# Transpositions of the heads: full-array sets at five places, or pairs on two row halves in one run

## The chip, the cores and the metric

One core of one Trainium2 chip runs the whole program. The metric is device time in microseconds, the median over the runs of one kernel; lower is better.

## The reference, cut to what matters

One decoder layer over 512 tokens with a model width of 2048: a branch of windowed attention beside a branch of gated DeltaNet, merged by gates. The change lies in the DeltaNet branch, which has 16 key heads and 32 value heads of 128 channels:

```python
d_qkv = causal_conv_silu(d_qkv, conv_w)
dq, dk, dv = jnp.split(d_qkv, [DN_KEY, 2 * DN_KEY], axis=-1)
...
dq = jnp.repeat(l2_norm(dq.reshape(B, T, DN_K_HEADS, DN_HEAD_K)), rep, axis=2)
dv = dv.reshape(B, T, DN_V_HEADS, DN_HEAD_V)
...
o = gated_delta_rule(dq, dk, dv, g, beta)
o = rms_norm(o, dn_norm_w) * jax.nn.silu(dz.reshape(B, T, DN_V_HEADS, DN_HEAD_V).astype(f32))
y_b = o.reshape(B, T, DN_VAL).astype(x.dtype) @ w_o_dn
```

`gated_delta_rule` works in chunks of 64 tokens: it inverts a triangular matrix per chunk and head and scans the chunks with a 128x128 state. Everything is float32.

## The kernel before, in words

**The stream.** The projections are computed channel by token: `channel_tile` makes one 128x512 tile of the output as 16 steps of three products each (`mm3`, lines 273 to 275: high part by high, high by low, low by high, 48 products of 128x512). Every second step calls `pump`, which advances all work that runs beside the stream; a tile so has 8 pumps, and 6 products lie between two pumps. The weights arrive by DMA as 1 MB tiles `raw` and are split in halves into a high part `whi` (cast, ScalarE, line 61) and a low part `wlo` (subtraction, VectorE, line 62); three halves are held, and a half lasts 24 products.

**The heads.** `delta_heads` goes through 16 groups, each of one key head with its two value heads. A group has five tiles of the stream: query, two values, two gates z. What follows on a tile is a Python generator (`queries`, `values`, `zgate`, and `scan` behind `queries`) that issues instructions and gives a number of pumps to wait with `yield`. [...]

**What is transposed.** The convolution leaves the query `yq` and the values `yv` as channels by tokens. `transpose4` (line 320) turns a 128x512 tile with four TensorE transpositions of 128x128: the data is the loaded operand, the identity `ident` the moving one. The query is transposed (`ptq`) only for the sum of its squares, ScalarE's `sumsq` (`junk`, line 793). The values (`ptv`) are scaled by `knorm` on ScalarE (line 927) into `vt`, four instructions for each value head. The scan's result `osb` (tokens by channels, two heads) is transposed back (`pto`) and multiplied by the gates `zh` on VectorE (line 1082), then stored to `o_d`. That makes five sets of four per group: one query, two values, two outputs.

**The block products.** `pu` holds products of 64x64 blocks that complete the inverse for a pair of chunks of 64 (lines 987, 988, 882). They run on four 64x64 tiles of the array at once: a matrix of float32 is two instructions, so a group has 32 of them. `block_copy` moves half of the result to `Y` for the next group.

**The scan.** For each of four pieces of 128 tokens: `pp` (state by key), `r`, `pv` (line 1026), its copy `vn` on ScalarE (line 1028), `vs` on VectorE (line 1033), then the products into `pod` (lines 1041, 1044, 1045) and from it the new state `S`, the copy `osb` and its squares.

**PSUM.** Each bank holds 128x512 float32. Two are for the stream, three for the pool `ptp` (transpositions, `pqk`, `pu`) and three for `psc` (the scan).

Of the kernel before, what the change touches and what calls it, by code (L numbers as in the profile page):

```python
# [7 lines left out]
F32 = mybir.dt.float32  # L8
F32R = mybir.dt.float32r
I32 = mybir.dt.int32  # L10
AF = mybir.ActivationFunctionType
ALU = mybir.AluOpType
AX = mybir.AxisListType
PSUM = bass.MemoryType.PSUM
DRAM = bass.MemoryType.DRAM

P = 128
T = 512
D = 2048
KT = D // P  # L20
NTB = T // P
EPS = 1e-6
KH = 16
VH = 32
QH = 32
HD = 64
# [19 lines left out]
class Layer:  # L46
# [653 lines left out]
    def delta_heads(self):  # L700
        tc, nc = self.tc, self.nc
        with ExitStack() as sb:
            self.ptp = sb.enter_context(tc.tile_pool(name="ptph", bufs=3, space=PSUM, reuse_waits="tile"))
            self.psc = sb.enter_context(tc.tile_pool(name="psch", bufs=3, space=PSUM, reuse_waits="tile"))
            self.gwk = sb.enter_context(tc.tile_pool(name="gwkh", bufs=1, reuse_waits="tile"))
            wk = sb.enter_context(tc.tile_pool(name="dnB", bufs=2, reuse_waits="tile"))
            self.tt = []
            for n in range(4):
                t = wk.tile([P, NTB, P], F32, tag=f"tt{n}", name=f"tt{n}", bufs=1)
                nc.gpsimd.memset(t[HD:P, :, 0:HD], 0.0)  # L710
                self.tt.append(t)
            while not self.solved:
                self.step_slow(self.solves)
            self.Y = None
            self.go(self.first_blocks(wk), 1)
            ws = sb.enter_context(tc.tile_pool(name="wsum", bufs=1, reuse_waits="tile"))
            sums = None
            for g in range(KH):
                if g == 3:
                    sums = self.paced(self.weight_sums(ws), 2.0)  # L720
                if g == 7:
                    self.drain_slow(self.solves)
                self.heads(wk, g)
            for j in range(9, 12):
                self.merge_gate("ma", j, self.ma_d)
            self.drain_live()
            self.drain_slow(sums)
# [156 lines left out]
    def block_copy(self, wk, pu):  # L884
# [2 lines left out]
        self.nc.vector.tensor_copy(out=Y[HD:P], in_=pu[1][HD:P])  # L887
        self.nc.vector.tensor_copy(out=Y[0:HD], in_=pu[0][HD:P])

    def first_blocks(self, wk):  # L890

        blk = self.block_load(wk, 0)
        yield 6
        pu = [self.ptp.tile([P, NTB, HD], F32, tag="tp", name="pu") for _ in range(2)]
        for c in range(NTB):
            self.block_product(pu, blk, c)
        self.block_copy(wk, pu)
# [9 lines left out]

    def zgate(self, wk, ps, st):
        nc = self.nc
        zh = wk.tile([P, T], F32, tag="z", name="zh", bufs=2)  # L910
        nc.scalar.activation(zh, ps, AF.Copy, scale=self.dnwh)
        th = wk.tile([P, T], F32, tag="th", name="zth")
        nc.scalar.activation(th, ps, AF.Tanh, scale=0.5)
        yield 1
        nc.vector.scalar_tensor_tensor(out=zh, in0=th, scalar=1.0, in1=zh, op0=ALU.add, op1=ALU.mult)
        st["z"].append(zh)

    def values(self, wk, g, e, ps, st):
        nc = self.nc
        y = wk.tile([P, T], F32, tag="y", name="yv", bufs=3)  # L920
        yield from self.conv(wk, ps, 32 + 2 * g + e, y)
        yield 3
        pt = self.ptp.tile([P, T], F32, tag="tp", name="ptv")
        self.transpose4(pt, lambda c: y[:, c * P : (c + 1) * P])
        vt = wk.tile([P, NTB, P], F32, tag="vt", name="vt", bufs=3)
        for c in range(NTB):
            nc.scalar.activation(vt[:, c, :], pt[:, c * P : (c + 1) * P], AF.Copy, scale=self.knorm[:, c, g : g + 1])
        st[f"v{e}"] = vt

    def queries(self, wk, g, ps, st):  # L930

        nc = self.nc
        sl = lambda c: slice(c * P, (c + 1) * P)
        q = wk.tile([P, T], F32, tag="y", name="yq", bufs=3)
        yield from self.conv(wk, ps, g, q)
        M = [self.decay_load(wk, 2 * g + e) for e in range(2)]
        kT = wk.tile([P, T], F32, tag="kT", name="kT")
        nc.sync.dma_start(out=kT, in_=self.kT_d[g])
        yield 2
        pt = self.ptp.tile([P, T], F32, tag="tp", name="ptq")  # L940
        self.transpose4(pt, lambda c: q[:, sl(c)])
        ss = self.sumsq(wk, pt)
        yield 3
        epsq = wk.tile([P, NTB], F32, tag="epsq", name="epsq")
        nc.vector.tensor_scalar(out=epsq, in0=ss, scalar1=EPS, scalar2=EPS * P, op0=ALU.add, op1=ALU.mult)
        yield 1
        for e in range(2):
            self.decay_mask(M[e])
        masks = self.last_mask
        ts1 = wk.tile([P, NTB, HD], F32, tag="ts1", name="ts1", bufs=1)  # L950
        qd, TT = [], []
        for e in range(2):
            h = 2 * g + e
            qe = wk.tile([P, NTB, P], F32, tag="qe", name="qe", bufs=2)
            nc.sync.dma_start(out=qe.rearrange("p c i -> p (c i)"), in_=self.eg_rows[h].partition_broadcast(P))
            qd.append(qe)
            b, hl = h // 16, h % 16
            t = self.tt[h % 4]
            for k2 in range(2):
                s = slice(k2 * HD, (k2 + 1) * HD)  # L960
                nc.sync.dma_start(out=t[s, :, s], in_=self.ts_d[b, k2, hl].rearrange("c j i -> j c i"))
            if e:
                nc.sync.dma_start(out=ts1[0:HD], in_=self.ts_d[b, 1, hl].rearrange("c j i -> j c i"))
            TT.append(t)
        while self.Y is None:
            yield 1
        Y = self.Y
        blk = self.block_load(wk, g + 1) if g + 1 < KH else None
        yield 3
        for e in range(2):  # L970
            self.decay_exp(M[e], 2 * g + e)
        k = wk.tile([P, NTB, P], F32, tag="k", name="k")
        nc.sync.dma_start(out=k.rearrange("p c d -> p (c d)"), in_=self.k_d[g])
        yield 1
        for e in range(2):
            qf = qd[e].rearrange("p c i -> p (c i)")
            self.behind(nc.gpsimd.tensor_tensor(out=qf, in0=qf, in1=q, op=ALU.mult), masks)  # L977
        yield 1
        pqk = self.ptp.tile([P, NTB, P], F32, tag="tp", name="pqk")
        for c in range(NTB):  # L980
            nc.tensor.matmul(pqk[:, c, :], lhsT=kT[:, sl(c)], rhs=q[:, sl(c)], start=True, stop=True)
        for e in range(2):
            nc.vector.tensor_tensor(out=M[e], in0=pqk, in1=M[e], op=ALU.mult)
        yield 4
        pu = [self.ptp.tile([P, NTB, HD], F32, tag="tp", name="pu") for _ in range(2)]
        for c in range(NTB):
            nc.tensor.matmul(pu[0][0:HD, c, :], lhsT=Y[HD:P, c, :], rhs=TT[0][HD:P, c, HD:P], start=True, stop=True)
            nc.tensor.matmul(pu[1][0:HD, c, :], lhsT=Y[0:HD, c, :], rhs=ts1[0:HD, c, :], start=True, stop=True)
            if blk:
                self.block_product(pu, blk, c)  # L990
        for e in range(2):
            nc.vector.tensor_tensor(
                out=TT[e][0:HD, :, HD:P],
                in0=pu[e][0:HD],
                in1=self.neg_beta[0:HD, :, 2 * g + e].unsqueeze(2).to_broadcast([HD, NTB, HD]),
                op=ALU.mult,
            )
        if blk:
            self.block_copy(wk, pu)
        yield 2  # L1000
        while "v1" not in st:
            yield 1
        yield 2
        yield from self.scan(wk, g, k, kT, TT, qd, M, epsq, st)

    def scan(self, wk, g, k, kT, TT, qd, M, epsq, st):
        nc = self.nc
        sl = lambda c: slice(c * P, (c + 1) * P)
        v = [st["v0"], st["v1"]]
        osb = wk.tile([P, 2, NTB, P], F32, tag="osb", name="osb", bufs=1)  # L1010
        osq = wk.tile([P, 2, NTB], F32, tag="osq", name="osq")
        S = None
        for c in range(NTB):
            if c:
                pp = self.psc.tile([P, 4, P], F32, tag="sc", name="pp")[:, 0:2, :]
                nc.tensor.matmul(pp, lhsT=kT[:, sl(c)], rhs=S, start=True, stop=True)  # L1016
                r = wk.tile([P, 2, P], F32, tag="r", name="r", bufs=1)
                for e in range(2):
                    nc.vector.scalar_tensor_tensor(
                        out=r[:, e, :], in0=pp[:, e, :], scalar=self.neg_eg[:, c, 2 * g + e : 2 * g + e + 1],  # L1020
                        in1=v[e][:, c, :], op0=ALU.mult, op1=ALU.add,
# [41 lines left out]
        z = st["z"]  # L1063
# [9 lines left out]
        for e in range(2):  # L1073
# [1 line left out]
            nc.vector.tensor_tensor(  # L1075
                out=of, in0=of, in1=ro[:, e * NTB : (e + 1) * NTB].unsqueeze(2).to_broadcast([P, NTB, P]), op=ALU.mult
            )
        yield 3
        for e in range(2):
            pt = self.ptp.tile([P, T], F32, tag="tp", name="pto")  # L1080
            self.transpose4(pt, lambda c: osb[:, e, c, :])
            nc.vector.tensor_tensor(out=z[e], in0=pt, in1=z[e], op=ALU.mult)
            yield 1
        yield 1
        for e in range(2):
# [767 lines left out]
```

## Time and profile before

| what | value |
|---|---|
| median of 3 runs | 2813.19 us (2806.18, 2813.19, 2815.07) |
| the profiled execution's own time | 2809.24 us |
| its span (first to last instruction) | 2807.4 us |
| granted TensorE clock over the span | 0.997 |
| TensorE busy | 2777.5 us |
| VectorE busy | 1951.0 us |
| ScalarE busy | 1207.4 us |
| stretch of the heads, with the tiles of the merge gate behind them | about 1018 to 2122 us |

Rows of the profile give the engine (PE TensorE products, PEld TensorE loads, DVE VectorE, ACT ScalarE, POOL GpSimd, SP the DMA queue), the line of the kernel, the operation, output<-inputs by the program's names with buffer numbers left out, the shape, and xN for a number of like instructions. In rows in order of time the first number is the start, the second how long it took, in us, and a bracket at the end gives an idle time before it with what ended it. In rows of groups the numbers behind the bar are busy us, the mean of one in ns, and behind a second bar the engine's idle time before them. For TensorE a row also has rows*columns of the array that are used. A row by stretches gives from:to, its length, then for PE, PEld, DVE, ACT and POOL the busy us and number of instructions, then the granted clock, the DMA engines' share and GB/s. A row of waits says who waited for whom, and the sum in us, the times, and the longest. Neighbouring products overlap, so what one costs in the row is told by the distance of starts.

### The profile page before, as it was taken

Reading aid. Unit: us, or ns where it says so; the run is one execution under the profiler, and the core shown is the slowest. Engines: PE = TensorE matmul, PEld = TensorE weight load, DVE = VectorE, ACT = ScalarE, POOL = GpSimd, SP = SyncE. Lnnn points to the kernel's source line nnn. Section 1 sums busy time; section 2 is a strip of 40 time slices with the busy share of each in tenths; the row PEclk is TensorE's granted clock in tenths of the full one; section 3 lists DMA queues with packets and bytes.
Section 4 is the critical chain, followed back from the end, with each engine's and each line's share of the span. In section 5 each row is a group of like instructions: output and inputs, shape, how many; then the busy total and the mean of one; then the engine's idle time right before and its main releaser. Section 6 shows DMA issues by size and latency. Waiting matters only on the chain.

```text
span 2807.4 us, 38312 instructions
## 1 busy us (share of the span) xinstructions
PE 2777.5 (99%) x14090; PEld 2271.1 (81%) x14090; DVE 1951.0 (69%) x3253; ACT 1207.4 (43%) x2508; POOL 144.3 (5%) x124
## 2 busy tenths in 40 slices
PE   8999999999999999999999999999999999999999
PEld 6788888877777778888888888888888788878887
DVE  7866976877758667678666666666657766664676
ACT  5554443244544433344534343434435454432443
POOL 0010100100100010000000000000000000000000
PEclk9999999999999999999999999999999999999999
DMA  9868763322252253367787667676657887885684
GB/s 403 350 235 252 255 237 132 111 78 98 86 165 98 91 170 119 118 210 245 248 260 251 227 234 249 222 245 221 230 184 244 305 299 248 295 274 184 243 318 165
DMA packets 228992, 603.38 MB, mean 215 GB/s; under 512 B 76706, under 2 KB 103074, under 8 KB 188482
## 3 DMA queue, kind: packets, MB, share of 16 engines
q1 hardware_dynamic: 228804, 600.93, 62.6%
q8 instruction: 111, 1.82, 0.3%
q14 instruction: 77, 0.63, 0.1%
HBM read 480.38 MB, written 118.24 MB: 213 GB/s over the span
## 4 chain that ended last, share of the span: by engine, by line
PE 89%; DMA 4%; DVE 3%; issue 1%; ACT 1%; POOL 0%; SPq 0%; DVEq 0%; POOLq 0%; ACTq 0%
PE mm L273 21%; PE mm L275 21%; PE mm L274 21%; PE m L274 5%; PE m L275 5%; PE m L273 5%; DMA E<-g_rows 1%; PE pv L1026 1%; PE pod L1045 1%; PE O L1560 1%; PE pod L1044 1%; PE pp L1016 1%; PE pod L1041 1%; DVE wlo L62 1%; DMA wa<-in_w_ada_ss 1%
## 5 line engine op out<-in xcount | busy, mean ns | idle before, releaser
L273 PE MATMUL mm<-hh,whi 128*128 128x512 f32 x2784 | 1125.7, 404 | 0.0
L275 PE MATMUL mm<-hh,wlo 128*128 128x512 f32 x2784 | 1090.1, 392 | 1.9 <-DVE wlo L62 1.9
L274 PE MATMUL mm<-hl,whi 128*128 128x512 f32 x2784 | 1087.7, 391 | 0.0
L62 DVE TENSOR_TENSOR wlo<-raw,whi 128x1024 fp32r<-128x1024 f32 x516 | 635.8, 1233 | 402.4 <-ACT whi L61 394.7
L61 ACT CAST whi<-raw 128x1024 fp32r<-128x1024 f32 x516 | 541.5, 1050 | 857.3 <-PE mm L274 613.1
L275 PEld LDWEIGHTS mm<-hh,wlo 128*128 128x128 f32 x2784 | 523.4, 188 | 116.4 <-DVE wlo L62 2.5
L273 PEld LDWEIGHTS mm<-hh,whi 128*128 128x128 f32 x2784 | 524.2, 188 | 113.8 <-issue 11.8
L274 PEld LDWEIGHTS mm<-hl,whi 128*128 128x128 f32 x2784 | 524.5, 188 | 102.2 <-issue 1.4
L1291 DVE TENSOR_TENSOR q<-q,q 128x1024 f32<-128x1024 f32 x96 | 124.6, 1298 | 0.9 <-DMA q<-in_w_out 0.9
L809 ACT ACTIVATE E<-E,neg_g 128x128 f32<-128x128 f32 x256 | 81.4, 391 | 92.7 <-POOL E L803 92.6
L847 DVE TENSOR_TENSOR A<-A,atmp 128x62 f32<-128x62 f32 (+30 forms) x124 | 107.5, 867 | 0.4
L839 DVE TENSOR_TENSOR atmp<-A 128x62 f32<-128x62 f32 (+30 forms) x124 | 106.8, 861 | 0.4
L977 POOL TENSOR_TENSOR qe<-qe,yq 128x512 f32<-128x512 f32 x32 | 52.7, 1666 | 907.2 <-DMA qe<-eg_rows 645.2
L1046 ACT COPY osb<-pod 128x256 f32<-128x256 f32 x64 | 23.8, 372 | 151.9 <-PE pod L1045 151.9
L803 POOL TENSOR_SCALAR_AFFINE_SELECT E<-E 128x512 f32<-128x512 f32 x64 | 60.0, 951 | 432.2 <-DMA E<-g_rows 367.0
L1028 ACT COPY vn<-pv 128x256 f32<-128x256 f32 x64 | 23.8, 372 | 115.5 <-PE pv L1026 115.5
L652 DVE SCALAR_TENSOR_TENSOR yv<-mm,convh,yv 128x511 f32<-128x511 f32 (+2 forms) x96 | 71.4, 743 | 1.6
L1528 ACT ACTIVATE sm<-sm,mx,rs 128x128 f32<-128x128 f32 x128 | 61.5, 482 | 3.7 <-DVE mx L1523 3.3
L1033 DVE TENSOR_SCALAR vs<-vn,kd 128x128 f32<-128x128 f32 x96 | 23.2, 283 | 53.7 <-ACT vn L1028 53.7
L472 DVE SCALAR_TENSOR_TENSOR wa<-wa,silu_cb 128x2048 f32<-128x2048 f32 x22 | 50.1, 2283 | 3.6 <-DMA wa<-in_w_ada_ss 3.6
L1056 DVE SCALAR_TENSOR_TENSOR S<-S,egl,pod 128x128 f32<-128x128 f32 x64 | 19.3, 342 | 47.9 <-ACT junk L1049 47.9
L1045 PE MATMUL pod<-vn,E 128*128 128x128 f32 x256 | 46.8, 275 | 0.0
(449 smaller groups left out, 3637.7 us busy)
## 6 DMA issues: line engine op xcount, KB each, us to landing
raw<-in_w_ch SPq DMA_DIRECT2D x158, 1024.0 KB
wa<-in_w_ada_ss SPq DMA_DIRECT2D x32, 1024.0 KB
q<-in_w_od SPq DMA_DIRECT2D x64, 512.0 KB
g_d<-q SPq DMA_DIRECT2D x64, 512.0 KB
raw<-g_d SPq DMA_DIRECT2D x32, 1024.0 KB
raw<-in_w_od SPq DMA_DIRECT2D x24, 1024.0 KB
gw<-in_w_ada_gate SPq DMA_DIRECT2D x16, 1024.0 KB
E<-g_rows SPq DMA_DIRECT2D x64, 256.0 KB
```

The lines of the kernel that those rows point to most:

```text
L61: h = self.nc.scalar.copy(out=hi, in_=src)
L62: l = self.nc.vector.tensor_tensor(out=lo, in0=src, in1=hi.bitcast(F32), op=ALU.subtract)
L273: nc.tensor.matmul(ps, lhsT=wh, rhs=xh, start=first, stop=False)
L274: nc.tensor.matmul(ps, lhsT=wh, rhs=xl, start=False, stop=False)
L275: self.last_mm = nc.tensor.matmul(ps, lhsT=wl, rhs=xh, start=False, stop=last)
L652: nc.vector.scalar_tensor_tensor(out=y[:, s:], in0=ps[:, : T - s], scalar=w[:, j : j + 1], in1=y[:, s:], op0=ALU.mult, op1=ALU.add)
L809: self.nc.scalar.activation(E[:, c, :], E[:, c, :], AF.Exp, bias=self.neg_g[:, c, h : h + 1])
L839: eng.tensor_tensor(out=t, in0=A[:, m : m + 1, m + 1 :].to_broadcast([P, m, n]), in1=A[:, :m, m : m + 1].to_broadcast([P, m, n]), op=ALU.mult,
L847: self.behind(eng.tensor_tensor(out=A[:, :m, m + 1 :], in0=A[:, :m, m + 1 :], in1=t, op=ALU.add))
L1045: nc.tensor.matmul(po[:, e, :], lhsT=M[e][:, c, :], rhs=vn[:, e, :], start=c == 0, stop=True)
L1291: self.behind(nc.vector.tensor_tensor(out=q[f], in0=q[x], in1=q[y], op=ALU.add))
L1528: nc.scalar.activation(t, t, AF.Exp, scale=r[:, h : h + 1], bias=mx[:, h : h + 1], accum_out=den[:, h : h + 1])
```

## The change

The five sets of full transpositions per group become pairs of half transpositions. `half_transposes` takes 64 rows of the data at a time: rows 0 to 63 on the upper half of the array into one PSUM bank, rows 64 to 127 on the lower half into another. Each loads 64 rows by 128 columns and moves a 64x64 identity. All of a group's sets stand in one run right behind its block products: 8 half transpositions of the query, 16 of the preceding group's outputs, 16 of the two values. Therefore:

- `values` leaves the convolved tile in `st`, and `queries` waits (in the program's order) until both value tiles and the preceding group's outputs are there.
- PSUM is shared out anew: `ptp` has two pairs of banks, `psc` two banks. `pu` and the query's halves share a pair, the outputs take both banks of `psc`.
- ScalarE reads both halves with one instruction, so their number stays: 8 scalings and 4 squares, now in one row. The product with the gates becomes four VectorE instructions of 128x256 instead of two of 128x512, and the gates get four buffers.
- The scan leaves `osb` and the gates in `outs`; the last group transposes its outputs in a run of their own.

```diff
-            self.ptp = sb.enter_context(tc.tile_pool(name="ptph", bufs=3, space=PSUM, reuse_waits="tile"))
-            self.psc = sb.enter_context(tc.tile_pool(name="psch", bufs=3, space=PSUM, reuse_waits="tile"))
+            self.ptp = sb.enter_context(tc.tile_pool(name="ptph", bufs=2, space=PSUM, reuse_waits="tile"))
+            self.psc = sb.enter_context(tc.tile_pool(name="psch", bufs=2, space=PSUM, reuse_waits="tile"))
...
+    def bank_pair(self, name):
+        return self.ptp.tile([P, 2, T], F32, tag="tp", name=name)
+
+    def half_transposes(self, dst, src, n):
+        for i in range(n):
+            for u in range(2):
+                s = slice(u * HD, (u + 1) * HD)
+                self.nc.tensor.transpose(dst(u)[:, i, :], src(i, s), self.ident[s, s])
+
+    def out_blocks(self, g):
+        osb, z = self.outs[g]
+        pt = [self.psc.tile([P, 4, P], F32, tag="sc", name="pto").rearrange("p a (b i) -> p (a b) i", i=HD) for _ in range(2)]
+        self.half_transposes(lambda u: pt[u], lambda i, s: osb[s, i // NTB, i % NTB, :], 2 * NTB)
+        return pt
+
+    def out_gates(self, g, pt):
+        osb, z = self.outs.pop(g)
+        for u in range(2):
+            for e in range(2):
+                zu = z[e].rearrange("p (c u i) -> p u c i", u=2, i=HD)[:, u]
+                self.nc.vector.tensor_tensor(out=zu, in0=pt[u][:, e * NTB : (e + 1) * NTB, :], in1=zu, op=ALU.mult)
...
-        pt = self.ptp.tile([P, T], F32, tag="tp", name="ptv")
-        self.transpose4(pt, lambda c: y[:, c * P : (c + 1) * P])
-        vt = wk.tile([P, NTB, P], F32, tag="vt", name="vt", bufs=3)
-        for c in range(NTB):
-            nc.scalar.activation(vt[:, c, :], pt[:, c * P : (c + 1) * P], AF.Copy, scale=self.knorm[:, c, g : g + 1])
-        st[f"v{e}"] = vt
+        st[f"y{e}"] = y
...
-        yield 2
-        pt = self.ptp.tile([P, T], F32, tag="tp", name="ptq")
-        self.transpose4(pt, lambda c: q[:, sl(c)])
-        ss = self.sumsq(wk, pt)
-        yield 3
...
+        while not ("y0" in st and "y1" in st and (not g or g - 1 in self.outs)):
+            yield 1
+        pair = self.bank_pair("pu")
...
+        ptq = pair[:, :, NTB * HD :].rearrange("p u (c i) -> p u c i", i=HD)
+        self.half_transposes(lambda u: ptq[:, u], lambda c, s: q[s, sl(c)], NTB)
+        pto = self.out_blocks(g - 1) if g else None
+        ptv = self.bank_pair("ptv").rearrange("p u (c i) -> p u c i", i=HD)
+        self.half_transposes(lambda u: ptv[:, u], lambda i, s: st[f"y{i // NTB}"][s, sl(i % NTB)], 2 * NTB)
...
+        if g:
+            self.out_gates(g - 1, pto)
...
-        for e in range(2):
-            pt = self.ptp.tile([P, T], F32, tag="tp", name="pto")
-            self.transpose4(pt, lambda c: osb[:, e, c, :])
-            nc.vector.tensor_tensor(out=z[e], in0=pt, in1=z[e], op=ALU.mult)
+        self.outs[g] = (osb, z)
+        if g == KH - 1:
+            yield 3
+            self.out_gates(g, self.out_blocks(g))
+        while g in self.outs:
             yield 1
```

TensorE's row of instructions in the middle of the heads, before: the second set of outputs (`pto`) with its neighbours of the stream, and further on the first value set behind the query-key products.

```order
L275 MATMUL mm<-hh,wlo 128x512
L320 MATMUL pto<-ident,osb 128x128 x4
L273 MATMUL mm<-hh,whi 128x512
L274 MATMUL mm<-hl,whi 128x512
L275 MATMUL mm<-hh,wlo 128x512
L273 MATMUL mm<-hh,whi 128x512
L274 MATMUL mm<-hl,whi 128x512
L275 MATMUL mm<-hh,wlo 128x512
L320 MATMUL pto<-ident,osb 128x128 x4
```

The same engine now, at a group's block products (the numbers behind `tt` and `ts` are buffers):

```order
L1005 MATMUL pu<-tt_9009,Y 64x64
L1006 MATMUL pu<-ts_11636,Y 64x64
L882 MATMUL pu<-ta,lab 64x64 x2
L899 MATMUL pu<-ident,yq 128x64 x8
L899 MATMUL pto<-ident,osb 128x64 x16
L899 MATMUL ptv<-ident,yv 128x64 x16
L273 MATMUL mm<-hh,whi 128x512
L274 MATMUL mm<-hl,whi 128x512
L275 MATMUL mm<-hh,wlo 128x512
```

The sets that stood each between products of the stream now follow the block products without a product of the stream between them; the query's halves are written beside `pu` and so bear its name.

ScalarE's row from the second value set to the scan's first piece, before (`zh` and `zth` belong to the gate tile, `vn`, `osb` and `junk` with `osq` to the scan):

```order
L61 CAST whi<-raw 128x1024
L927 ACTIVATE vt<-ptv,knorm 128x128 x4
L911 ACTIVATE zh<-mm,dnwh 128x512
L913 ACTIVATE zth<-mm 128x512
L1028 COPY vn<-pv 128x256
L61 CAST whi<-raw 128x1024
L1046 COPY osb<-pod 128x2x128
L1049 ACTIVATE junk,osq<-pod 128x128 x2
```

And now:

```order
L61 CAST whi<-raw 128x1024 x2
L938 ACTIVATE zh<-mm,dnwh 128x512
L940 ACTIVATE zth<-mm 128x512
L1026 ACTIVATE vt<-ptv,knorm 128x128 x8
L1035 ACTIVATE junk,ss<-pu 128x128 x4
L61 CAST whi<-raw 128x1024
L1065 COPY vn<-pv 128x256
L1083 COPY osb<-pod 128x2x128
L1086 ACTIVATE junk,osq<-pod 128x128 x2
```

Both value sets and the query's squares stand together, and the cast of a half of the weights, which stood behind the scan's first copy `vn`, stands ahead of it. VectorE's row at the same place, before:

```order
L62 TENSOR_TENSOR wlo<-raw,whi 128x1024
L915 SCALAR_TENSOR_TENSOR zh<-zth,zh 128x512
L1033 TENSOR_SCALAR vs<-vn,kd 128x128 x2
L62 TENSOR_TENSOR wlo<-raw,whi 128x1024
L1053 COPY S<-pod 128x256
```

And now (line 914 is the product of outputs and gates):

```order
L887 COPY Y<-pu 64x256
L914 TENSOR_TENSOR zh<-pto,zh 128x4x64 x4
L888 COPY Y<-pu 64x256
L942 SCALAR_TENSOR_TENSOR zh<-zth,zh 128x512
L1050 TENSOR_SCALAR epsq<-ss 128x4
L62 TENSOR_TENSOR wlo<-raw,whi 128x1024
L1070 TENSOR_SCALAR vs<-vn,kd 128x128 x2
L1090 COPY S<-pod 128x256
```

The difference of the weights (`wlo`) has moved from behind the scan's `vs` to ahead of it.

More of the change, by code (lines that the diff above doesn't have):

```diff
@@ L713, in delta_heads @@
                 self.step_slow(self.solves)
-            self.Y = None
+            self.Y, self.outs = None, {}
             self.go(self.first_blocks(wk), 1)
@@ L893, in first_blocks @@
         yield 6
-        pu = [self.ptp.tile([P, NTB, HD], F32, tag="tp", name="pu") for _ in range(2)]
+        pair = self.bank_pair("pu")
+        pu = [pair[:, u, 0 : NTB * HD].rearrange("p (c i) -> p c i", i=HD) for u in range(2)]
         for c in range(NTB):
@@ L909, in zgate @@
         nc = self.nc
-        zh = wk.tile([P, T], F32, tag="z", name="zh", bufs=2)
+        zh = wk.tile([P, T], F32, tag="z", name="zh", bufs=4)
         nc.scalar.activation(zh, ps, AF.Copy, scale=self.dnwh)
@@ L938, in queries @@
         nc.sync.dma_start(out=kT, in_=self.kT_d[g])
-        yield 2
-        pt = self.ptp.tile([P, T], F32, tag="tp", name="ptq")
-        self.transpose4(pt, lambda c: q[:, sl(c)])
-        ss = self.sumsq(wk, pt)
-        yield 3
-        epsq = wk.tile([P, NTB], F32, tag="epsq", name="epsq")
-        nc.vector.tensor_scalar(out=epsq, in0=ss, scalar1=EPS, scalar2=EPS * P, op0=ALU.add, op1=ALU.mult)
-        yield 1
+        yield 6
         for e in range(2):
@@ L978, in queries @@
         yield 1
-        pqk = self.ptp.tile([P, NTB, P], F32, tag="tp", name="pqk")
+        pqk = self.bank_pair("pqk")[:, 0].rearrange("p (c i) -> p c i", i=P)
         for c in range(NTB):
@@ L984, in queries @@
         yield 4
-        pu = [self.ptp.tile([P, NTB, HD], F32, tag="tp", name="pu") for _ in range(2)]
+        while not ("y0" in st and "y1" in st and (not g or g - 1 in self.outs)):
+            yield 1
+        pair = self.bank_pair("pu")
+        pu = [pair[:, u, 0 : NTB * HD].rearrange("p (c i) -> p c i", i=HD) for u in range(2)]
         for c in range(NTB):
@@ L997, in queries, with scan @@
             )
+        if g:
+            self.out_gates(g - 1, pto)
+        v = [wk.tile([P, NTB, P], F32, tag="vt", name="vt", bufs=3) for _ in range(2)]
+        for c in range(NTB):
+            for e in range(2):
+                nc.scalar.activation(
+                    v[e][:, c, :].rearrange("p (u i) -> p u i", u=2), ptv[:, :, e * NTB + c, :], AF.Copy,
+                    scale=self.knorm[:, c, g : g + 1],
+                )
         if blk:
             self.block_copy(wk, pu)
[L1000 to L1006, printed above, removed]
+        ss = wk.tile([P, NTB], F32, tag="ss", name="ss")
+        for c in range(NTB):
+            junk = wk.tile([P, P], F32, tag="junk", name="junk", bufs=1)
+            nc.scalar.activation(
+                junk.rearrange("p (u i) -> p u i", u=2), ptq[:, :, c, :], AF.Square, accum_out=ss[:, c : c + 1]
+            )
+        yield 3
+        yield from self.scan(wk, g, k, kT, TT, qd, M, ss, v, st)
+    def scan(self, wk, g, k, kT, TT, qd, M, ss, v, st):
         nc = self.nc
         sl = lambda c: slice(c * P, (c + 1) * P)
-        v = [st["v0"], st["v1"]]
         osb = wk.tile([P, 2, NTB, P], F32, tag="osb", name="osb", bufs=1)
@@ L1013, in scan @@
         for c in range(NTB):
+            if c == 1:
+                epsq = wk.tile([P, NTB], F32, tag="epsq", name="epsq")
+                nc.vector.tensor_scalar(out=epsq, in0=ss, scalar1=EPS, scalar2=EPS * P, op0=ALU.add, op1=ALU.mult)
             if c:
@@ L1077, in scan @@
             )
-        yield 3
-        for e in range(2):
-            pt = self.ptp.tile([P, T], F32, tag="tp", name="pto")
-            self.transpose4(pt, lambda c: osb[:, e, c, :])
-            nc.vector.tensor_tensor(out=z[e], in0=pt, in1=z[e], op=ALU.mult)
+        self.outs[g] = (osb, z)
+        if g == KH - 1:
+            yield 3
+            self.out_gates(g, self.out_blocks(g))
+        while g in self.outs:
             yield 1
```

## The prediction

> **What bounds the kernel now.** I read the page first (busy shares and the chain that ended last), then busy time by stretches, then TensorE's waits inside the stretch that the change touches, 1018 to 2122 us, where the heads run.
>
> ```profile
> span 2807.4 us, 38312 instructions
> PE 2777.5 (99%) x14090; PEld 2271.1 (81%) x14090; DVE 1951.0 (69%) x3253; ACT 1207.4 (43%) x2508; POOL 144.3 (5%) x124
> PE 89%; DMA 4%; DVE 3%; issue 1%; ACT 1%; POOL 0%; SPq 0%; DVEq 0%; POOLq 0%; ACTq 0%
> 1018.00:2122.00 1104.00, 1098.63 (x5840) 918.83 (x5839) 744.94 (x1222) 453.37 (x1111) 81.27 (x62) 1.00 0.64 215
> PE pto L320 <- DVE osb L1075: 2.9, 2, 2.2
> PE pp L1016 <- DVE S L1053: 1.2, 1, 1.2
> PE ptv L320 <- DVE yv L659: 0.9, 1, 0.9
> PE ptq L320 <- DVE yq L659: 0.4, 1, 0.4
> ```
>
> TensorE is the bound: in the stretch it is busy 1098.6 of 1104 us at the full granted clock (1.00), with 5.4 us of waits in four places (us, times, longest). VectorE stands at 745 us and ScalarE at 453. So time is won or lost by what the transpositions cost in TensorE's row of instructions, and by new waits. That cost is read from starts, since durations overlap:
>
> ```profile
> 1047.12 0.40 PE L275 MATMUL mm<-hh,wlo 128*128 128x512 f32 x1
> ...
> 1050.53 0.39 PE L275 MATMUL mm<-hh,wlo 128*128 128x512 f32 x1
> ...
> 1050.95 0.22 PE L987 MATMUL pu<-tt,Y 64*64 64x64 f32 x1
> ...
> 1051.30 0.22 PE L987 MATMUL pu<-tt,Y 64*64 64x64 f32 x1
> ...
> 1051.47 0.50 PE L273 MATMUL mm<-hh,whi 128*128 128x512 f32 x1
> ...
> 1052.97 0.39 PE L273 MATMUL mm<-hh,whi 128*128 128x512 f32 x1
> 1105.09 0.39 PE L275 MATMUL mm<-hh,wlo 128*128 128x512 f32 x1
> 1105.32 0.60 PE L320 MATMUL pto<-ident,osb 128*128 128x128 f32 x4
> 1105.68 0.48 PE L273 MATMUL mm<-hh,whi 128*128 128x512 f32 x1
> ...
> 1106.92 0.39 PE L275 MATMUL mm<-hh,wlo 128*128 128x512 f32 x1
> 768.54 0.61 PE L1491 MATMUL S<-kd,aq 64*128 64x128 f32 x8
> ```
>
> The first two rows are 15 products apart: 3.41/15 = 0.227 us, the step of the large products. Around the four transpositions at 1105.32, 1105.09 to 1106.92 holds six such steps (1.36) and 1.83 us passed: a stop costs 0.47 us. Four transpositions take 0.60 with the last one's 0.272 (its row stands below), so their step is 0.328/3 = 0.109 us: 0.44 of the 0.47 is the transpositions themselves, and only 0.03 the stop. Around the block products 1050.53 to 1052.97 holds seven steps (1.59) and 2.44 passed: 0.85 us. There four 64x64 tiles start together, and six rounds take 1051.30 - 1050.95, or 0.058 us each; eight rounds make 0.47, and 0.38 goes to leaving and entering the full array. The last row is the nearest to the new form: attention's products on two row halves with 128 columns. Eight instructions, four pairs, take 0.61; less one duration (0.27) three pair steps are left: 0.11 us. Two halves do run together.
>
> **The change part by part.** *Removed:* per group four stops' worth of transpositions in five sets of four: query, two values, two outputs. In the row of instructions before, the query set stands right behind the scan's products and one value set right behind the query-key products; these two pay only 4 x 0.109 = 0.44, the other three 0.47. Per group 2.28 us, over 16 groups 36.5 us.
>
> *Added:* per group 20 pairs of half transpositions (four of the query, eight of the outputs, eight of the values); all in all 320 pairs. The price of a pair isn't in the trace. It is bounded by how long one half loads its data and moves the identity:
>
> ```profile
> L320 PEld LDWEIGHTS pto<-ident,osb 128*128 128x128 f32 x128 | 15.7, 140 | 7.5 <-DVE osb L1075 3.7
> L638 PEld LDWEIGHTS pr<-ident,EG 128*32 128x32 f32 x4 | 0.4, 97 | 0.0
> L981 PEld LDWEIGHTS pqk<-yq,kT 128*128 128x128 f32 x128 | 16.7, 191 | 1.3
> L882 PEld LDWEIGHTS pu<-ta,lab 64*64 64x64 f32 x256 | 8.7, 134 | 0.4 <-issue 0.4
> L1016 PE MATMUL pp<-S,kT 128*128 128x256 f32 x96 | 28.5, 378 | 1.2 <-DVE S L1053 1.2
> L320 PE MATMUL ptv<-ident,yv 128*128 128x128 f32 x128 | 19.2, 272 | 0.9 <-DVE yv L659 0.9
> L882 PE MATMUL pu<-ta,lab 64*64 64x64 f32 x256 | 10.9, 224 | 0.0
> ```
>
> The means are in ns. An ordinary load takes 191 for 128 columns and 134 for 64, 0.89 per column; a transposition's takes 140 for 128 columns and 97 for 32, 0.45 per column. The moving side takes 378 for 256 columns and 272 for 128: 0.83 per column, whatever the operation. So today's step of 0.109 is the 128 columns of the identity (106 ns), with the load (58) hidden under it. A half transposition moves 64 columns (53 ns) but still loads 128 (58 ns). With the two halves together a pair costs no less than 0.058, the round of the 64x64 tiles, and no more than 0.110, attention's pair, which moves 128 columns and loads them at the ordinary rate. I take 0.063: the load's 58 plus the 5 by which the 64x64 round stands above its 53 of moving. It is nearest to the lower end because both things that make attention's pair long are halved here. 320 x 0.063 = 20.2 us (18.6 to 35.2).
>
> [...]
>
> *Entering another tiling:* the run goes from 64x64 tiles to 64x128 tiles. No row shows that; below it is nothing, above half of the 0.38 that the block products pay for two changes, 0.19. I take 0.10, 1.6 us over 16 groups (0 to 3.0). The last group's outputs come in a stop of their own, which pays the 0.38 instead of two times 0.03: 0.3 us.
>
> So TensorE's row: 36.5 - 20.2 - 1.6 - 0.3 = 14.4 us less.
>
> *The waits.* Of TensorE's four waits shown first, those on osb, yv and yq, 4.2 us together, stand at transpositions that now come 24 large products or more behind their data; I count 3 us of them as gone, the rest as moved. The generators' new loop, which holds a group's block products until both value tiles and the last outputs are there, waits in the program's order only: it puts the block products 30 large products later and the scan 6 later; the drain at the end of the heads is not longer, since both outputs now go in one step.
>
> *ScalarE behind the run.* Eight scalings of the values and four squares of the query, which stood at three places, now stand in one row ahead of a cast of the next weights and the scan's first copy.
>
> ```profile
> 1045.46 1.14 ACT L927 ACTIVATE vt<-ptv,knorm 128x128 f32<-128x128 f32 x4
> 1032.24 0.28 ACT L793 ACTIVATE junk<-ptq 128x128 f32<-128x128 f32 x1
> 1032.64 0.28 ACT L793 ACTIVATE junk<-ptq 128x128 f32<-128x128 f32 x1
> 1062.26 0.37 ACT L1028 COPY vn<-pv 128x256 f32<-128x256 f32 x1 [2.09 <-PE pv L1026]
> 1063.41 1.05 ACT L61 CAST whi<-raw 128x1024 fp32r<-128x1024 f32 x1 [0.78 <-PE mm L274]
> 1061.62 0.60 PE L1026 MATMUL pv<-vt,tt 128*128 128x128 f32 x4
> 1064.81 0.60 PE L1041 MATMUL pod<-vs,k 128*128 128x256 f32 x2
> 1062.67 0.48 DVE L1033 TENSOR_SCALAR vs<-vn,kd 128x128 f32<-128x128 f32 x2 [1.65 <-ACT vn L1028]
> 1064.50 1.22 DVE L62 TENSOR_TENSOR wlo<-raw,whi 128x1024 fp32r<-128x1024 f32 x1 [1.35 <-ACT whi L61]
> ```
>
> A scaling takes 0.26 from start to start ((1.14 - 0.37)/3), a square with its read 0.40: 8 x 0.26 + 4 x 0.40 = 3.7 us. The cast can begin only when 18 large products behind the run have freed its buffer, 18 x 0.227 + 0.2 = 4.3 us; so the row is over in time. Then comes what is new: cast, its difference on VectorE (L62), and only then the scan's vs, where before vs came first. From the first product of pv: cast begins at about 0, the difference at 1.1, vs ends at 1.1 + 1.2 + 0.5 = 2.8; pod, which reads vs, starts 1064.81 - 1061.62 = 3.2 later. 0.4 us of slack stays, and I count 1 us of waits over the 16 groups (0 to 7: the slack gone in each group and another 0.4 lost). VectorE gets four products of 128x256 for two of 128x512, about 0.3 us more per group on an engine that is busy two thirds of the stretch; the scan's next needs lie behind the 0.4 us just counted. [...] POOL's work is the same.
>
> Sum: 14.4 + 3 - 1 = 16.4 us less than the profiled execution, whose own time is 2809.2 us (2 us around its span). The median of the three runs is 2813.2, 4 us above it. 2813.2 - 16.4 = 2797 us. About 0.3%, 8.4 us, is what a measurement of this kernel can tell from no change.
>
> **Rivals.** (1) The load sets the pair: 0.110 us, as in attention. Then 320 pairs cost 35.2 us, TensorE's row is 35.2 + 1.9 - 36.5 = 0.6 us longer, and with 2 us of waits won 1.4 us are left: 2812. For it: the nearest form on record costs just that. Against it: the shorter loads of transpositions, if they are as short on 64 rows. [...] Chance 0.18.
>
> (2) Slower: the two halves of a transposition don't run together, since no transposition on row halves is on record. Each half then costs 0.063 to 0.109, a pair 0.126 to 0.218; the gain of 36.5 + 2 - 1.9 is used up at 0.114 us a pair, and from 0.141 on the kernel is slower by over 8.4 us. At two full steps, 0.218, 320 pairs take 69.8: 2813.2 + 33 = 2846. Against it: attention's halves overlap. Chance 0.07.
>
> (3) ScalarE's row is late: if scalings and squares cost their durations (0.37 and 0.47) and not their steps, the row lasts 4.8 us and the cast is 0.5 late, the 0.4 of slack is gone and 0.1 to 0.5 us per group is waited for at pod, 2 to 8 us. With the other terms kept, 9 to 15 us are won: 2798 to 2804. It is a part of my case's range.
>
> [...]
>
> **How the numbers follow.** My case 0.75, rival 1 0.18, rival 2 0.07. My case alone reaches from 2786 (pairs at 0.058, no price for the tiling, all 5.4 us of waits gone, 23 us won, and 4 us more for the spread of the runs shown) to 2808 (pairs at 0.075, 3 us for the tiling, 7 us of waits: 5 us won). To keep no more than 2 in 10 outside, the range takes in rival 1: 2786 to 2813. Faster by over 0.3% (below 2804.8): nearly all of my case, 0.71. Within 0.3%: the rest of it, rival 1 and the least of rival 2, 0.22. Slower: 0.07.
>
> **What would show it.** Right: pairs of half transpositions 0.06 us apart, one stop of about 0.85 + 0.1 + 20 x 0.063 = 2.2 us per group, no set of four transpositions in the heads, loads of about 140 ns on 64 rows, TensorE's busy time in the stretch about 14 us less, no wait of TensorE at pod above 0.1 us. Wrong: loads of 190 ns and pairs at 0.11, or halves that start one behind the other; or TensorE waiting for vs in every group.

## The result, and the profile after

| | before | after |
|---|---|---|
| median | 2808.35 us (6 runs, 2806.18 to 2815.07) | 2789.47 us (6 runs, 2787.87 to 2791.69) |
| ratio, 95% interval | | 0.9929 (0.9916 to 0.9941) |
| profiled execution: span | 2807.4 us | 2787.2 us |

The changed kernel is faster by 18.9 us, 0.7%. The forecast was 2797 us (2786 to 2813). With three more runs the median of before is 4.8 us lower than the one that the forecast started from.

The head of the page of after: the span and the engines' busy time. Then TensorE's waits in the stretch of the heads (who waited for whom: us, times, longest), and the row of that stretch, which ends 20 us earlier than in before.

```profile
span 2787.2 us, 38923 instructions
PE 2759.0 (99%) x14410; PEld 2256.5 (81%) x14410; DVE 1957.9 (70%) x3285; ACT 1207.4 (43%) x2508; POOL 137.9 (5%) x124
PE pod L1078 <- DVE vs L1070: 2.0, 2, 1.5
PE pp L1053 <- DVE S L1090: 0.9, 1, 0.9
1018.00:2102.00 1084.00, 1081.11 (x6161) 905.15 (x6160) 753.17 (x1254) 453.42 (x1111) 74.97 (x62) 1.00 0.65 219
```

TensorE is still the bound. In the heads it is busy 17.5 us less (1098.63 before) and waits 2.9 us where it waited 5.4. The waits on osb, yv and yq are gone; new is the one on vs, which the list shows in two of the 16 groups. (Delays that leave TensorE no idle time aren't in the list; three more of these come up below.)

Where the time went can be read by counting. The stream's tiles `mm` are 8352 large products in all kernels here, so the n-th of them is the same work in each. From the 3337th to the 7507th, which holds the heads, 1148.50 us pass in before and 1128.48 in after. That is 20.0 of the 20.2 us by which the spans differ.

Within the heads most groups are free of waits. One group is 240 large products, here from the product ahead of one group's block products to that of the next: the first two rows are before, the next two after.

```profile
1588.22 0.39 PE L275 MATMUL mm<-hh,wlo 128*128 128x512 f32 x1
1654.63 0.39 PE L275 MATMUL mm<-hh,wlo 128*128 128x512 f32 x1
```

```profile
1582.08 0.39 PE L275 MATMUL mm<-hh,wlo 128*128 128x512 f32 x1
1647.43 0.39 PE L275 MATMUL mm<-hh,wlo 128*128 128x512 f32 x1
```

66.41 us before, 65.35 after: 1.06 us a group, about 17 us over 16 groups. The rest is waits, which come further down, less 0.4 for the two ends: the first group has no outputs to transpose, and the last ones need a stop of their own, which costs 0.87 us.

The run itself, TensorE's row of after in order of time (start and duration in us):

```profile
1251.52 0.39 PE L275 MATMUL mm<-hh,wlo 128*128 128x512 f32 x1
...
1252.47 0.46 PE L899 MATMUL pu<-ident,yq 64*128 64x64 f32 x8
1252.77 0.66 PE L899 MATMUL pto<-ident,osb 64*128 64x64 f32 x16
1253.27 0.67 PE L899 MATMUL ptv<-ident,yv 64*128 64x64 f32 x16
1253.86 0.50 PE L273 MATMUL mm<-hh,whi 128*128 128x512 f32 x1
...
1255.59 0.39 PE L274 MATMUL mm<-hl,whi 128*128 128x512 f32 x1
```

Sixteen halves of the outputs, eight pairs, take 1253.27 - 1252.77: 0.0625 us a pair. From 1251.52 to 1255.59 there are eight steps of the large products (8 x 0.227 = 1.82) and 4.07 us passed, so the whole stop costs 2.25 us. The block products alone cost 0.84 in before. That leaves 1.41 us for 20 pairs, of which 1.25 are the pairs and 0.16 the entry into the other tiling.

### The profile page after: what moved, and what is told of

Read it like the earlier page. It is cut to its first block, busy times and chain, and to the rows that moved or that the text cites. A ratio compares the mean times of both kernels' runs of the same rounds, so it can differ in the third digit from the quotient of the medians.

```text
span 2787.2 us, 38923 instructions
## 1 busy us (share of the span) xinstructions
PE 2759.0 (99%) x14410; PEld 2256.5 (81%) x14410; DVE 1957.9 (70%) x3285; ACT 1207.4 (43%) x2508; POOL 137.9 (5%) x124
## 4 chain that ended last, share of the span: by engine, by line
PE 90%; DMA 3%; DVE 3%; ACT 1%; issue 1%; SPq 0%; POOL 0%; DVEq 0%; POOLq 0%; ACTq 0%
PE mm L273 22%; PE mm L275 22%; PE mm L274 21%; PE m L274 5%; PE m L275 5%; PE m L273 5%; PE pod L1082 1%; PE pv L1063 1%; PE O L1597 1%; PE pp L1053 1%; PE pod L1078 1%; PE pod L1081 1%; DVE wlo L62 1%; DMA gw<-in_w_ada_gate 1%; DMA prev<-yo_d 1%
## 5 line engine op out<-in xcount | busy, mean ns | idle before, releaser
L62 DVE TENSOR_TENSOR wlo<-raw,whi 128x1024 fp32r<-128x1024 f32 x516 | 636.1, 1233 | 463.8 <-ACT whi L61 450.7
L1056 DVE SCALAR_TENSOR_TENSOR r<-pp,neg_eg,vt 128x128 f32<-128x128 f32 x96 | 29.2, 345 | 34.3 <-PE pp L1053 34.1
L657 ACT ACTIVATE th<-yv 128x512 f32<-128x512 f32 x32 | 20.2, 632 | 70.6 <-DVE yv L652 70.5
```

The costliest lines, as they stand in the source:

```text
L62: l = self.nc.vector.tensor_tensor(out=lo, in0=src, in1=hi.bitcast(F32), op=ALU.subtract)
```

## The experiments

The durations are medians; all ratios are to the kernel before, run on the same chip. Before took 2807.79 us beside the first four experiments and 2810.61 beside the last two, so a difference from after's median, which was taken beside 2808.35, is good to some 2 us.

### One run, but full transpositions

```diff
-        self.half_transposes(lambda u: ptq[:, u], lambda c, s: q[s, sl(c)], NTB)
+        for c in range(NTB):
+            nc.tensor.transpose(ptq[:, c // 2, c % 2, :], q[:, sl(c)], self.ident)
```

and likewise for outputs and values; the readers' layouts follow, everything else is as in after.

> The five sets of a group stay full transpositions of 128x128, but stand in the changed kernel's place, in one run behind the block products. My theory (the halves win, because a pair takes 0.063 us and a full transposition 0.109; the stops are worth only 0.03 us each): the stop at the block products costs 0.84 + 20 x 0.109 = 3.0 us instead of 2.24, so about 12 us above the changed kernel and 6 us below the kernel before (2 us of stops, 1.5 us of cheaper stops of the scan, 2.5 us of waits). Rival (the one run wins, the halves are incidental): within 4 us of the changed kernel, that is 15 to 20 us below before.

Measured: 2798.82 us, ratio 0.9965 (0.9953 to 0.9978). It is 9 us below before and 9.4 above after. TensorE's row at one group:

```profile
1584.93 0.39 PE L275 MATMUL mm<-hh,wlo 128*128 128x512 f32 x1
...
1586.37 1.04 PE L907 MATMUL pto<-ident,osb 128*128 128x128 f32 x8
1587.24 1.04 PE L1015 MATMUL ptv<-ident,yv 128*128 128x128 f32 x8
...
1651.01 0.39 PE L275 MATMUL mm<-hh,wlo 128*128 128x512 f32 x1
```

Eight full transpositions take 0.87 us, 0.109 each, as in before; a group takes 66.08 us. So the halves bring 66.08 - 65.35 = 0.73 us a group, 11.7 us in all, and the run alone 0.33, 5.3 us. The run gains more than that in this kernel, since the list shows no wait of TensorE in its heads, and by the stops less than 1 us of waits is left. Both parts of the change earn their place. The halves are the larger part of the gain of a group without waits, but not of the whole: from the 3337th to the 7507th large product 1135.99 us pass here, so of the 20.0 us the run with full transpositions brings 12.5 and the halves the other 7.5, because after has more waits than this kernel.

### Halves, but at the old five places

```diff
-        pt = self.ptp.tile([P, T], F32, tag="tp", name="ptv")
-        self.transpose4(pt, lambda c: y[:, c * P : (c + 1) * P])
+        pt = self.half_set("ptv", lambda c, s: y[s, c * P : (c + 1) * P])
```

`half_set` makes four pairs into two banks; query and outputs likewise, in the kernel before, with PSUM shared out as in after.

> Pairs of half transpositions, but in sets of four at the five old places, each between products of the stream or of the scan, with the changed kernel's PSUM pools. My theory (entering and leaving another tiling of the array costs about 0.38 us, which the block products' run pays anyway): a set costs 4 x 0.063 + 0.38 = 0.63 us instead of 0.44 to 0.47, five sets 0.85 us more per group, 14 us over 16 groups, less 1.5 for the scan's stops: about 12 us above before. Rival (the halves win wherever they stand): a set costs 0.28, about 14 us below before.

Measured: 2824.15 us, ratio 1.0058 (1.0042 to 1.0073), 16.4 us slower than before. A set of outputs in TensorE's row:

```profile
1583.94 0.39 PE L275 MATMUL mm<-hh,wlo 128*128 128x512 f32 x1
1584.26 0.46 PE L899 MATMUL pto<-ident,osb 64*128 64x64 f32 x8
...
1585.94 0.39 PE L275 MATMUL mm<-hh,wlo 128*128 128x512 f32 x1
```

Six steps are 1.36 us and 2.00 passed: a set of four pairs alone costs 0.64 us, where the four full transpositions cost 0.47. Of it 4 x 0.0625 = 0.25 are the pairs and 0.39 is leaving and entering the full array, the 0.38 that the prediction read from the block products. So here the cheaper pair is worth nothing by itself; it pays only in a stop that has already changed the tiling (1.41 us for 20 pairs in after, where the five sets cost 2.35 in before). A group without waits takes 67.24 us (from 1596.25 to 1663.49, ahead of the block products), 0.83 more than in before, or 13.3 us in all; the rest is longer waits, 7.6 us in the heads where before has 5.4.

### One half behind the other

```diff
-        for i in range(n):
-            for u in range(2):
+        for u in range(2):
+            for i in range(n):
```

> The changed kernel with the loops of the half transpositions exchanged: within a set all upper halves first, then all lower halves, so neighbours use the same half of the array. My theory (the two halves of a pair run at the same time, which is half of the gain): a half by itself takes 0.063 us, 40 of them 2.5 us instead of 1.25, so 20 us above the changed kernel, about the time before. If load and moving of one half don't overlap either, 0.11 each and 50 us above. Rival (the order within a set doesn't matter, because TensorE takes loads ahead): within 3 us of the changed kernel.

Measured: 2795.15 us, ratio 0.9955 (0.9941 to 0.9968), 5.7 us above after. Neither theory's number holds: by the same count the stop costs 2.65 us here and 2.25 in after. TensorE's row in one run:

```profile
1584.43 0.47 PE L899 MATMUL pu<-ident,yq 64*128 64x64 f32 x8
1584.73 0.78 PE L899 MATMUL pto<-ident,osb 64*128 64x64 f32 x13
1585.29 0.27 PE L899 MATMUL ptv<-ident,yv 64*128 64x64 f32 x1
1585.35 0.22 PE L899 MATMUL pto<-ident,osb 64*128 64x64 f32 x1
1585.41 0.22 PE L899 MATMUL ptv<-ident,yv 64*128 64x64 f32 x1
1585.41 0.22 PE L899 MATMUL pto<-ident,osb 64*128 64x64 f32 x1
```

The query's eight halves, written as four upper and four lower, still take 0.30 us (1584.43 to 1584.73), as in pairs. With eight of a half in a row they no longer all find a partner. In each of the 15 groups whose run holds all three sets the first four upper halves of `pto` start alone, 0.063 us apart, and the first lower half starts right behind the fifth (0.007 us). So a half by itself steps as a pair does (0.0625 in after): the two halves of a pair run at the same time, as the theory said. What the theory missed is that most halves find a partner all the same. The values' upper halves (`ptv`, 1585.29), which are written behind all of `pto`, start ahead of the last three lower halves of `pto` (1585.35, 1585.41, 1585.47). Going by the source's order, TensorE here started a product on the free half of the array ahead of three earlier ones for the other half, in both places, so in this run its row was not run strictly in order. The query's four halves of a kind all found a partner. The trace has no record of the order in which the products were issued; that it is the source's is argued from the four that run alone. A reach beyond three was not tested.

### Each half as an ordinary product

```diff
-                self.nc.tensor.transpose(dst(u)[:, i, :], src(i, s), self.ident[s, s])
+                self.nc.tensor.matmul(dst(u)[:, i, :], lhsT=src(i, s), rhs=self.ident[s, s], start=True, stop=True)
```

It moves the same 64 columns, but is two instructions, each with an ordinary load.

> The changed kernel with every half transposition written as an ordinary float32 product of the data with the identity: same operands, 64 rows, 128 columns loaded, 64 moved, but two instructions each and the ordinary load (0.89 ns per column instead of 0.45). My theory (the load sets the pair): a pair of instructions takes 0.11 us, a pair of products 0.22, so 320 x 0.16 = 51 us above the changed kernel, about 32 above before. Rival (moving 64 columns sets it): 0.058 a pair of instructions, 0.116 a pair of products, 17 us above the changed kernel.

Measured: 2838.15 us, ratio 1.0107 (1.0093 to 1.0121), 48.7 us above after. The loads of the values' halves here (minimum, median, maximum in ns), then a set in TensorE's row:

```profile
L899 PEld LDWEIGHTS ptv<-ident,yv x512: 188/188/188, 1060.1 to 2090.6; 64*128 64x128 f32 x171
1607.02 1.95 PE L899 MATMUL pto<-ident,osb 64*128 64x64 f32 x32
1608.81 1.95 PE L899 MATMUL ptv<-ident,yv 64*128 64x64 f32 x32
```

and the same loads in after:

```profile
L899 PEld LDWEIGHTS ptv<-ident,yv x256: 137/139/142, 1057.2 to 2042.6; 64*128 64x128 f32 x128
```

Thirty-two instructions, 16 pairs, take 1.79 us: 0.112 a pair, against 0.0625, with the same columns moved. So it is the load that sets the step: 188 ns against 139 for the same 64 rows and 128 columns. The block products say the same: ordinary too, with 64 columns moved but only 64 loaded, they step by 0.058 us. A pair of ordinary loads costs what attention's pair costs (0.11), which was the first rival's price; transpositions escape it because their load is shorter.

### The outputs of the kernel before, three pumps later

This one asks what a wait of TensorE costs. In before the longest one in the heads stands at the first set of outputs. Its rows in TensorE's order:

```profile
1173.15 0.39 PE L273 MATMUL mm<-hh,whi 128*128 128x512 f32 x1
1175.77 0.66 PE L320 MATMUL pto<-ident,osb 128*128 128x128 f32 x4 [2.24 <-DVE osb L1075]
...
1176.91 0.77 PE L275 MATMUL mm<-hh,wlo 128*128 128x512 f32 x1
1177.48 0.63 PE L273 MATMUL mm<-hh,whi 128*128 128x512 f32 x1
...
1179.62 0.63 PE L275 MATMUL mm<-hh,wlo 128*128 128x512 f32 x1
1180.04 0.48 PE L273 MATMUL mm<-hh,whi 128*128 128x512 f32 x1
```

and the same place by stretches (from:to, length, busy us of PE, PEld, DVE, ACT and POOL, then the granted clock):

```profile
1174.00:1176.00 2.00, 0.23 (x2) 0.23 (x3) 2.00 (x3) 0.45 (x2) 0.00 (x0) 1.00 0.00 0
1176.00:1177.00 1.00, 1.00 (x10) 0.97 (x8) 1.00 (x2) 0.00 (x0) 0.00 (x0) 0.90 0.51 106
1178.00:1179.00 1.00, 1.00 (x4) 0.80 (x3) 0.56 (x1) 0.00 (x0) 0.00 (x0) 0.50 1.06 442
1180.00:1182.00 2.00, 2.00 (x15) 1.83 (x14) 0.13 (x1) 1.21 (x2) 0.00 (x0) 0.94 0.40 146
```

One us after the wait ended, the granted clock falls to 0.50 and stays there until about 1180.2, some 3.4 us. The large products step by 0.427 us instead of 0.227. The two sets' stops cost 2.81 and 2.14 us instead of 0.47 each: 4.0 us for a wait of 2.24.

```diff
-        yield 3
+        yield 6
         for e in range(2):
             pt = self.ptp.tile([P, T], F32, tag="tp", name="pto")
```

> The kernel before, with its outputs' two sets three pumps (18 large products, 4.1 us) later. In the profile of before, TensorE waits 2.24 us for osb at 1173.4 and 0.7 us a group later; behind the first wait the granted clock is 0.50 from about 1176.8 to 1180.2, and the two stops there cost 2.81 and 2.14 us instead of 0.47 each. Theory: the wait costs its idle time and then 1.8 us more, because it halves the clock behind it; with the data there in time both go, 4.0 + 0.9 = 4.9 us, the span falls from 2807.4 to about 2802.5 and no stretch in the heads has a clock under 1. Rival 1: the half clock has another cause at that place (the DMA engines are busy there at a share of 1.0) and stays at about 1177; then 2.9 us go. Rival 2: the outputs block the stream at another place, and the waits return there: no change within 1 us.

Measured: 2805.96 us, ratio 0.9982 (0.9972 to 0.9991), 4.7 us less by the medians. The same place by stretches, and TensorE's waits in the heads:

```profile
1175.00:1180.00 5.00, 5.00 (x29) 4.23 (x29) 4.83 (x8) 3.63 (x7) 0.00 (x0) 1.00 0.20 64
1180.00:1185.00 5.00, 5.00 (x28) 4.22 (x27) 5.00 (x8) 1.44 (x5) 0.00 (x0) 1.00 0.50 198
PE ptv L320 <- DVE yv L659: 1.4, 1, 1.4
PE pto L320 <- DVE zh L1082: 1.0, 3, 0.4
PE pp L1016 <- DVE S L1053: 0.8, 1, 0.8
PE ptq L320 <- DVE yq L659: 0.3, 1, 0.3
```

Wait and half clock are both gone, so the first rival falls; 1.0 us of new waits on zh have come, as the second rival said of a part. The heads take 1144.77 us, 3.7 less than in before. The span expected for the profiled execution was missed: at 2809.9 us it was the slowest of this kernel's ten runs. In it TensorE waits 2.3 us for a difference of the weights (L62) behind the heads, with the half clock behind that, so here the heads and the ratio are what counts.

That the wait causes the half clock rests on all eight profiles. Of TensorE's waits over 0.9 us behind the first 100 us, the four from 2.03 to 2.30 us are all followed by the half clock, of seven from 1.87 to 2.01 us two are, and of thirty up to 1.77 us none. One and the same wait shows both: for `wlo` at 850 us it is 1.87 us long in before and in after, and in before alone the clock falls.

The traces of before and after show what goes with it. Their record of the granted clock has stretches that all last a whole number of times 3.413 us, up to the last one (behind the first 37 us 239, 1, 94, 1 and 476 times in before, 806 times in after). So in both the clock changed on a grid of 3.413 us only. The wait for `wlo` by the windows of this grid, before first and then after:

```profile
849.13:852.54 3.41, 1.54 (x11) 1.03 (x6) 3.41 (x7) 3.04 (x5) 0.00 (x0) 1.00 0.04 7
852.54:855.96 3.42, 3.42 (x9) 2.69 (x9) 3.42 (x7) 0.00 (x0) 1.28 (x1) 0.50 0.52 125
848.24:851.65 3.41, 1.80 (x24) 1.04 (x24) 3.41 (x3) 3.41 (x10) 0.00 (x0) 1.00 0.00 0
851.65:855.06 3.41, 3.15 (x14) 2.59 (x15) 3.41 (x9) 1.13 (x2) 0.00 (x0) 1.00 0.27 38
```

In before the whole wait lies in one window, which so has 1.87 us without a product, and the next is at 0.50. In after 0.26 us of it fall into the next window; 1.61 are left, and the clock stays. In these two traces, from 100 us on, four windows have 1.87 us or more of TensorE idle (1.87, 2.24 and, 6 us from the end, 2.00 in before; the last whole one, 3.41, in after), and each is followed by 0.50. None with 1.61 us or less is; between the two figures neither trace has a window.

### The scan two pumps later

```diff
-        yield 3
+        yield 5
         yield from self.scan(wk, g, k, kT, TT, qd, M, ss, v, st)
```

An attempt on what waits are left in after.

> The changed kernel, with the scan two pumps (12 large products, 2.7 us) further behind the run of transpositions. What is left of TensorE's waits in the heads of the changed kernel, pod for vs (2.0 us in two places) and pp for S (0.9 us), costs 3.7 us by the stops (pod 2.59 and 1.68 instead of 0.90, pp 1.59 instead of 0.47, and 0.07 twice). Theory: vs is late there because ScalarE's row and the weights' difference stand ahead of it; 2.7 us more cover both waits at pod, some 2.5 us are won, span about 2784.5. Rival: the scan's end, 2.7 us later, delays the outputs and the next run, and the waits move there: no change within 1 us, or a loss of a few us.

Measured: 2798.04 us, ratio 0.9955 (0.9940 to 0.9970), 8.6 us above after by the medians, though before was 2.3 us higher on this chip. TensorE's loads waiting in the heads, and the waits at pod:

```profile
PEld pp L1053 <- DVE S L1090: 6.6, 14, 0.5
PE pod L1078 <- DVE vs L1070: 2.2, 2, 1.2
```

The theory falls and the rival stands: of the two waits at pod one stands in the same group as in after (at 1266.77, 1.02 us), the other has moved from the fifth group to the seventh, and in 14 groups one of the scan's pp now waits up to 0.5 us for its state S. The heads take 1130.54 us, 2.1 more than in after. The span is 6.9 us longer (2794.1), and most of the rest stands right behind the heads, where TensorE waits for the weights' difference and again loses its clock:

```profile
2127.23 0.50 PE L275 MATMUL mm<-hh,wlo 128*128 128x512 f32 x1 [2.23 <-DVE wlo L62]
2127.20:2132.20 5.00, 4.97 (x15) 3.93 (x16) 5.00 (x13) 1.22 (x3) 0.00 (x0) 0.66 0.76 235
```

Why vs is late in after can be seen, though. ScalarE's and VectorE's rows at the longest wait:

```profile
1258.61 0.28 ACT L1035 ACTIVATE junk<-pu 128x128 f32<-128x128 f32 x1 [2.46 <-DVE Y L888]
1260.07 1.04 ACT L61 CAST whi<-raw 128x1024 fp32r<-128x1024 f32 x1
1261.14 1.23 DVE L62 TENSOR_TENSOR wlo<-raw,whi 128x1024 fp32r<-128x1024 f32 x1 [0.54 <-ACT whi L61]
1262.29 0.47 DVE L1070 TENSOR_SCALAR vs<-vn,kd 128x128 f32<-128x128 f32 x2
```

The query's squares wait 2.46 us for VectorE's copy of the block products, which share their banks; then come cast, difference and vs, and pod starts at 1262.91, 1.47 us late. Where nothing delays it, in ten of the 16 groups, vs ends 0.51 us ahead of pod; pod never starts less than 0.15 us behind it, so 0.36 us of slack is left. In three groups that are not in the list of waits (pod at 1722.66, 1788.20 and 1853.86) this slack is used up too: the squares wait 0.7 us for the same copy, and another VectorE instruction of 1.2 us (line 1328) stands ahead of the difference. TensorE doesn't fall idle there, but each of these stops costs 0.2 us more.

## Why the prediction was right, point by point

**The removed sets** were put at 2.28 us a group. Read in the same way over a group without waits (a stop runs until the step is 0.227 again), they cost 0.94 for both outputs, 0.49 for one value set, and 0.48 and 0.44 for the sets behind other short products: 2.35.

**The pair of halves**, 0.063 between bounds of 0.058 and 0.110, measured 0.0625, and for the reason given: a load of 139 ns on 64 rows, 140 on 128. The ordinary products show that the load sets it. The 5 ns that the prediction added to the load's 58 were taken over from the block products; no run shows what they are, so the third digit is luck. Rival 1 needed loads of 190 ns; rival 2 needed halves that don't overlap. The halves' loads came near 190 only as ordinary products (188 ns), and there a pair stepped in 0.112 us.

**The entry into the other tiling**, taken as 0.10 between 0 and 0.19, is 0.16: 2.4 us in place of 1.6. It is below half of the 0.38 that the block products pay for two changes.

**TensorE's row** was to lose 14.4 us. By these stops it loses 16 x (2.35 - 1.41), or 15, less 0.4 at the ends: 14.6.

**The waits** are the term that was mis-sized: 3 us gone and 1 new, 2 in all. I priced a wait by its length in the list of waits. By their stops those of before cost 7.8 us where 5.4 are listed, 1.8 of the difference being the half clock behind one of them; those of after cost 4.6, of which 0.6 are the three unlisted ones at pod and 0.4 are six stops of `pp` that are 0.04 to 0.07 us longer. (The 3.7 in what was expected of the later scan left out all of the former and most of the latter.) That is 3.2 us in place of 2. The new wait came by the chain that the third rival named, cast, difference and vs, but not by the length of ScalarE's row, and not in each group: in five, where VectorE's other work held back the squares' release or the difference. The 0.4 us of slack that the prediction reckoned is there elsewhere (0.36). Its forecast of a wait at pod of no more than 0.1 us was wrong.

**What was missing.** The scan's own stops became cheaper, though no line of them changed. In a group without waits they cost 0.93, 1.38 and 0.475 us before (`pod` with 6 and with 10 instructions, `pp`) and 0.90, 1.35 and 0.469 after; with two of the 10s and three `pp` that is 0.12 us a group, 1.9 us in all. All five kernels with the run show it, the one with halves at the old places does not, although its PSUM is shared out as in after; so the number of banks is not the cause. What is stays open.

Together 14.6 + 3.2 + 1.9 = 19.7 us, for the 20.0 measured in the heads. The predicted 16.4 was short by the last two terms. By the medians the gain is 18.9, 2.5 us more than predicted; the other 4.8 of the 7.3 us by which the sum (2796.8) lay above the result are its start, 2813.2 as the median of three runs, for 2808.4 of six. The profiled execution, 2809.2, was the better start.

## What to carry to other kernels

Small work in another tiling cost less per piece here than on the full array (0.0625 us against 0.109), but a stop for it paid 0.38 us to leave the full array and come back; so collect it behind work that has already paid, and count the pieces: four pairs alone lost 0.17 us, twenty in such a stop won 0.94 (1.41 for 2.35). Price an operation by the step from start to start, and find out whether load or moving side sets it: here half the moved columns with an ordinary load brought nothing (0.112 us for a pair of instructions, against 0.109), with the shorter load of a transposition they did (0.0625). And read a wait of the bounding engine by what its stop costs over one without a wait: the half clock behind a wait of 2.24 us cost 1.8 us more, and the three delays of 0.2 us without idle time are in no list of waits.

## What was not expected of the hardware

- In before and after the granted clock of TensorE changed on a grid of 3.413 us only. From 100 us on, the windows with 1.87 us or more without a product were followed by 0.50, those with 1.61 or less were not. A wait of 2.24 us cost 4.0 us in before. Of the two waits of 1.87 us for `wlo`, the one that lay in one window (before) was followed by the half clock, the one that was split into 1.61 and 0.26 (after) was not.
- Where all upper halves were written ahead of the lower ones, TensorE started products on one row half ahead of three for the other half that stand earlier in the source: `ptv` at 1585.29 ahead of `pto` at 1585.35 to 1585.47.
- Of 64 rows and 128 columns of float32 an ordinary product's load took 188 ns and a transposition's 139, and a pair stepped in 0.112 and 0.0625 us.
